# A delta-rule recurrence with eight heads of a direction in one chain instead of two chains of four

## The chip, the core and the metric

The kernel runs on one core of a Trainium2 chip. The core's engines are PE (matrix multiply, with the load of its weights, PEld, shown apart), DVE, ACT and POOL (elementwise work) and SP, which here only issues transfers. Each engine takes its instructions in the order in which they were written down, and they meet through semaphores. The metric is the device time of one execution in microseconds (us), and less is better.

## What is computed

The program is a small network: two mixed layers and two blocks more. The change touches one part of the first layer, a recurrence over 768 tokens (256 of context, 512 of image), run once forwards and once backwards, for eight heads of 64 values each. For each head and token the reference does this to a 64 x 64 state S:

```python
def step(S, inp):
    r_t, w_t, k_t, v_t, kk_t, a_t = inp
    sa = jnp.einsum('bhvk,bhk->bhv', S, kk_t)
    S = (S * w_t[:, :, None, :] - sa[..., None] * (kk_t * a_t)[:, :, None, :]
         + v_t[..., None] * k_t[:, :, None, :])
    return S, jnp.einsum('bhvk,bhk->bhv', S, r_t)
```

The outputs of both directions are added. Beside it the layer has a softmax attention with four heads, which needs nothing of the recurrence.

## The kernel before

The 768 tokens are cut into 12 chunks of 64, so a direction takes 12 steps. Within a step the token-by-token rule is turned into matrix products of 64 x 64. The part of a step that needs no state is the generator `local` (line 1286); the part that needs the state of the step before is `state` (line 1378). The eight heads of a direction stand as four pairs, with the two heads of a pair on partitions 0 to 63 and 64 to 127. A chain is one direction `d` and one group `g` of two pairs (four heads), so there are four chains, and a tile of a chain is 128 partitions by 2 x 64 columns.

`local` goes so: ACT takes two exponentials of the cumulated decay, DVE and POOL scale the inputs into `AR` and `BK` (lines 1301 to 1306), PE multiplies `BK` by `AR` into one PSUM bank, and DVE masks it first into `W`, then into `G` (lines 1321 to 1323). Then the inverse of a triangular matrix is built by levels: three rounds that make `X` (line 1327), and for each of two levels a product `LT` by `X` that DVE masks into `W` (line 1351), and three rounds that make `XT` (line 1360), with a transpose by the unit matrix before and after (`turn`). Every round is one group of matmuls (`both`: all heads of the chain, 64 x 64 each) whose result DVE or ACT carries from PSUM into SBUF, where the next group of the same chain reads it. In the trace a 64 x 64 matmul of float32 shows as two instructions, so a group of a chain is 8 instructions in it. `LT`, `W` and the other tiles that live for the whole stage are cut from three slots named `room`, PSUM tiles are named `m`, and the inputs come from DRAM (`rkv`) by one DMA for each chain and step.

The order of all this work is made by a planner (`Plan.run`, with costs that are written down in it). It holds a list of streams: the modulation matmuls (`pmod`) and the attention (`attn0`) with priority 0, the four `states` with 1, the four `locals_` with 2. A stream is run to its next `yield`; it is ready again 150 ns after the planned end of what it issued. The planner takes the ready stream of the best priority, and where none is ready, the one that will be so first. The attention is spread over the stage by `pace`, which lets its next part start 1,900 ns of planned time after the one before (lines 932 and 1032). A PSUM tile takes one of seven banks in turn, whatever its size (line 1256).

Of the kernel before, what the change touches and what calls it, by code (L numbers as in the profile page):

```python
# [17 lines left out]
P = 128  # L18
# [476 lines left out]
class Kern:  # L495
# [623 lines left out]
    def rwkv_cols(self, col, done):  # L1119
# [15 lines left out]
        self.rkv = self.dp.tile([12, 2, P, 5, 128], F32, name="rkv")  # L1135
# [31 lines left out]
        def head(h):  # L1167
# [34 lines left out]
            for n, t in enumerate((r, kx, v, kk, b)):  # L1202
                nc.sync.dma_start(self.rkv[:, h // 2, :, n, 64 * (h % 2) : 64 * (h % 2) + 64].rearrange("c p i -> p c i"), t.rearrange("p (c i) -> p c i", i=64))
# [10 lines left out]
    def rwkv_steps(self, rw, extra, qkv):  # L1214
# [5 lines left out]
        two = lambda m: m.unsqueeze(1).to_broadcast([P, 2, m.shape[1]])  # L1220
        I = self.mk[:, :64]
# [8 lines left out]
        mN = [two(mk(d, 192, 64)) for d in range(2)]  # L1230
        mW = [[None] + [mk(d, 128 + 128 * l, 128).rearrange("p (a b) -> p a b", a=2).unsqueeze(1).to_broadcast([P, 2, 2, 64]) for l in (1, 2)] for d in range(2)]

        E = [self.ident[:, j] for j in J]
        dg = [(d, g) for g in range(2) for d in range(2)]
# [6 lines left out]

        room = [self.slot("room", a=1)[:, 0, :] for _ in range(3)]
        ARs = {}
        for n, x in enumerate(dg):
            t = self.wp.tile([P, 1024], F32, tag=("whi", "wlo")[n % 2], name=self.nm("AR"), bufs=2)
            nc.gpsimd.memset(t, 0.0)
            ARs[x] = [t[:, a : a + 512].rearrange("p (a b) -> p a b", a=2) for a in (0, 512)]
        nc.gpsimd.memset(room[0], 0.0)
        LTs, Ws, KDs, ins = {}, {}, {}, {}
        for n, x in enumerate(dg):  # L1250
            t = [room[0][:, 768 * n + a : 768 * n + a + 256].rearrange("p (a b) -> p a b", a=2) for a in (0, 256, 512)]
            LTs[x], Ws[x] = t[:2], t[2]
            KDs[x] = [room[1][:, 512 * n + a : 512 * n + a + 256].rearrange("p (a b c) -> p a b c", a=2, b=2) for a in (0, 256)]
            ins[x] = room[2][:, 640 * n : 640 * n + 640].rearrange("p (n h i) -> p n h i", n=5, h=2)
# [5 lines left out]
        def pairs(dst, lhs, rhs, start=True, stop=True):  # L1260

            for h, j in HJ:
                mm(dst[J[j], h, :], lhs(h, j), rhs(h, j), start=start, stop=stop)
# [6 lines left out]
        def both(dst, lhs, rhs, **k):  # L1270

            for h, j in HJ:
                mm(dst[J[j], h, :], lhs[:, h, J[j]], rhs[:, h, :], start=True, stop=True)
# [6 lines left out]
        def ct(d, g, tag, shape, bufs=1):  # L1280
            return self.kp.tile([P] + shape, F32, tag=f"{tag}{d}{g}", name=self.nm(tag), bufs=bufs)

        def load(i, d, g):
            nc.scalar.dma_start(ins[d, g], self.rkv[order[d][i], g].rearrange("p n (h i) -> p n h i", h=2))

        def local(i, d, g):
# [4 lines left out]
            hs = slice(2 * g, 2 * g + 2)  # L1291
            r, kx, v, kk, b = (ins[d, g][:, n, :, :] for n in range(5))
            Dp = dp[d][i % 2][:, hs, :]
            Din, Dex = (Dp[:, :, 1:65], Dp[:, :, 0:64]) if d == 0 else (Dp[:, :, 0:64], Dp[:, :, 1:65])
            Dc = Dp[:, :, 64:65] if d == 0 else Dp[:, :, 0:1]
            nc.scalar.activation(Din, cum[d][:, hs, cs], AF.Exp, scale=-C0)
            Di = ct(d, g, "X", [2, 64], 2)
            nc.scalar.activation(Di, cum[d][:, hs, cs], AF.Exp, scale=C0)
            AR, BK = ARs[d, g][i % 2], ct(d, g, "BK", [2, 128])
            LT, W = LTs[d, g][i % 2], Ws[d, g]  # L1300
# [7 lines left out]
            UV = ct(d, g, "UV", [2, 2, 64], 2)  # L1308
# [7 lines left out]
            G = ct(d, g, "G", [2, 2, 128], 2)  # L1316
            gp = bank().rearrange("p (a b) -> p a b", a=2)
            for h, j in HJ:
                mm(gp[J[j], h, :], BK[:, h, J[j]], AR[:, h, :], start=True, stop=True)
            A = [slice(64, 128), slice(0, 64)]  # L1320
            for j in range(2):
                nc.vector.tensor_tensor(W[J[j], :, J[j]], gp[J[j], :, 64 + 64 * j : 128 + 64 * j], mN[d][J[j]], op=MUL)
            nc.vector.tensor_tensor(G, gp.rearrange("p a (b c) -> p a b c", b=2), mG[d], op=MUL)
            yield

            I2 = two(I)
            for it in range(3):
                ps = ps1()
                if it == 0:
                    both(ps, W, I2)  # L1330
                else:
                    both(ps, W, X)
                X = ct(d, g, "X", [2, 64], 2)
                nc.vector.tensor_tensor(X, I2, ps, op=SUB)
                if it == 0:
                    if i < 11:
                        load(i + 1, d, g)
                    for j in range(2):
                        nc.scalar.copy(LT[J[j], :, J[j]], G[J[j], :, j, A[j]])
                elif it == 1:  # L1340

                    KD = KDs[d, g][i % 2]
                    ps = bank()[:, :256]
                    for h, j in HJ:
                        mm(ps[J[j], h * P : (h + 1) * P], BK[:, h, J[j]], self.ident, start=True, stop=True)
                    nc.scalar.copy(KD.rearrange("p a b c -> p (a b c)"), ps)
                yield
            for l in (1, 2):
                ps = ps1()
                both(ps, LT, X)  # L1350
                nc.vector.tensor_tensor(W.rearrange("p a (b c) -> p a b c", b=2), ps.unsqueeze(2).to_broadcast([P, 2, 2, 64]), mW[d][l], op=MUL)
                if l == 1:
                    pt = ps1()
                    turn(pt, X)
                    XT = DT = ct(d, g, "XT", [2, 64], 3)
                    nc.scalar.copy(DT, pt)
                else:
                    DT = XT
                yield
                for it in range(3):  # L1360
                    ps = ps1()
                    both(ps, W, XT)
                    if it == 2 and l == 2:
                        for j in range(2):
                            nc.vector.tensor_tensor(LT[J[j], :, J[j]], DT[J[j]], ps[J[j]], op=SUB)
                    else:
                        XT = ct(d, g, "XT", [2, 64], 3)
                        nc.vector.tensor_tensor(XT, DT, ps, op=SUB)
                    yield
                if l == 1:  # L1370
                    pt = ps1()
                    turn(pt, XT)
                    X = ct(d, g, "X", [2, 64], 2)
                    nc.scalar.copy(X, pt)
                    yield
            parts[i, d, g] = (c, cs, Dc, AR, G, UV, KD, LT)

        def state(i, d, g):

            c, cs, Dc, AR, G, UV, KD, T = parts.pop((i, d, g))  # L1380
            hs = slice(2 * g, 2 * g + 2)
            s0 = S.get((d, g))

            ps = ps1()
            for h in range(2):
# [4 lines left out]
            R = ct(d, g, "R", [2, 64])  # L1390
# [7 lines left out]
            if i < 11:  # L1398
                ps = ps1()
                pairs(ps, lambda h, j: KD[:, h, j, :], lambda h, j: UV[:, h, j, :])  # L1400
                Sn = ct(d, g, "S", [2, 64], 2)
                if s0 is None:
                    nc.vector.tensor_tensor(Sn, ps, Dc.to_broadcast([P, 2, 64]), op=MUL)
                else:
                    nc.vector.tensor_tensor(Sn, s0, ps, op=ADD)
                    nc.vector.tensor_tensor(Sn, Sn, Dc.to_broadcast([P, 2, 64]), op=MUL)
                S[d, g] = Sn
                yield
            ps = ps1()
            for h in range(2):  # L1410
# [5 lines left out]
            if (c, g) in seen:  # L1416
                nc.vector.tensor_tensor(cum[0][:, hs, cs], cum[seen[c, g]][:, hs, cs], ps, op=ADD)
            else:
                nc.scalar.copy(cum[d][:, hs, cs], ps)
                seen[c, g] = d  # L1420
            ended[d, g] = i + 1
            yield

        def locals_(d, g):
            load(0, d, g)
            for i in range(12):
                yield Wait(lambda: ended.get((d, g), 0) >= i - 1)
                yield from local(i, d, g)

        def states(d, g):  # L1430
            for i in range(12):
                yield Wait(lambda: (i, d, g) in parts)
                yield from state(i, d, g)

        self.run((extra, 0), (self.attn0(qkv, bank), 0), *[(states(*x), 1) for x in dg], *[(locals_(*x), 2) for x in dg])
# [1087 lines left out]
```

## Time and profile before

| what | us |
|---|---|
| median of three timed runs (3727.8 to 3730.7) | 3727.83 |
| the profiled execution, as timed | 3725.59 |
| its span on the core | 3723.8 |
| the stage of the recurrence, from its first input DMA (301.5) to its last matmul (772.3) | 470.8 |
| PE, PEld, DVE, ACT and POOL busy in that stage | 433.6, 359.8, 384.1, 303.3, 139.0 |

The profile is one execution. Busy times count what an engine executes. Matmuls overlap, and their ends are modelled, so a busy PE may still have gaps between the starts of its matmuls; PEld, with one weight load for every matmul, shows more of them. All lines of the kernel go through a recording helper and stand as L245, so instructions are told apart by the names of their tiles: `XT<-XT,m` is the DVE operation that makes `XT` from PSUM, `m<-XT,room` the matmuls that read it next.

### The profile page before, as it was taken

How to read it: one execution, taken by the hardware profiler on the slowest of the kernel's cores; microseconds unless marked ns; L12 is line 12 of the kernel's file. 1: busy time of each engine (PE TensorE's matmuls, PEld its weight loads, DVE VectorE, ACT ScalarE, POOL GpSimd, SP SyncE). 2: the span in 40 equal slices, each digit the busy share in tenths (PEclk: the TensorE clock that was granted, in tenths of full speed). 3: DMA queues.
4: the chain of work that ended last, by engine and by line, in shares of the span. 5: the costliest groups of instructions: out<-in, count | busy, mean ns of one | idle time of the engine just before them, and what ended most of it. 6: DMA issues, size and time to landing. Idle time of an engine off the chain costs nothing.

```text
span 3723.8 us, 61572 instructions
## 1 busy us (share of the span) xinstructions
PE 3541.7 (95%) x25118; PEld 2940.9 (79%) x25118; DVE 2124.9 (57%) x3764; ACT 1539.6 (41%) x2992; POOL 652.1 (18%) x817
## 2 busy tenths in 40 slices
PE   7998998999999998888899989999999999999998
PEld 5786787888999997766788867777888777778886
DVE  5636787865333346588644465656554456565542
ACT  5425666634212214355432333554433245543331
POOL 3314232202000002443300030003110100031100
PEclk9999999999999999988999999999999999999999
DMA  5423311123333312111232232223333322233322
GB/s 205 115 81 134 121 53 35 36 91 112 125 108 125 102 63 86 54 35 35 91 99 98 97 104 71 66 74 102 96 96 101 123 68 68 69 104 95 98 96 89
DMA packets 128860, 337.11 MB, mean 91 GB/s; under 512 B 41537, under 2 KB 44609, under 8 KB 127425
## 3 DMA queue, kind: packets, MB, share of 16 engines
q1 hardware_dynamic: 113168, 297.31, 24.8%
q10 hardware_dynamic: 13584, 29.57, 2.5%
q0 software_dynamic: 1824, 6.29, 0.5%
q8 instruction: 198, 3.24, 0.4%
q14 instruction: 86, 0.70, 0.1%
HBM read 315.30 MB, written 17.83 MB: 89 GB/s over the span
## 4 chain that ended last, share of the span: by engine, by line
PE 67%; DVE 8%; POOL 2%; ACT 2%; issue 1%; DMA 0%; ACTq 0%; DVEq 0%; POOLq 0%
PE g L245 60%; PE m L245 6%; DVE t L245 3%; POOL t L245 1%; PE pmod L245 1%; DVE G L245 1%; DVE wlo L245 1%; DVE X L245 1%; ACT t L245 0%; DVE pk L245 0%; DVE QF L245 0%; ACT whi L245 0%; DVE KF L245 0%; POOL X L245 0%; ACT pk L245 0%
## 5 line engine op out<-in xcount | busy, mean ns | idle before, releaser
L245 PE MATMUL g<-pk,whi 128*128 128x512 f32 x3328 | 1083.5, 398 | 21.0 <-ACT t L245 11.2
L245 ACT CAST whi<-raw 128x1024 fp32r<-128x1024 f32 (+1 forms) x441 | 460.0, 1043 | 1248.9 <-PE g L245 1169.8
L245 PE MATMUL g<-H,whi 128*128 128x512 f32 (+2 forms) x2976 | 746.6, 359 | 19.6 <-ACT H L245 9.7
L245 DVE TENSOR_TENSOR wlo<-raw,whi 128x1024 fp32r<-128x1024 f32 (+1 forms) x414 | 511.4, 1235 | 427.5 <-ACT whi L245 423.0
L245 PEld LDWEIGHTS g<-pk,whi 128*128 128x128 f32 x3328 | 623.1, 190 | 161.1 <-ACT t L245 12.3
L245 PE MATMUL g<-pk,wlo 128*128 128x512 f32 x1824 | 718.3, 394 | 2.0 <-DVE wlo L245 2.0
L245 PEld LDWEIGHTS g<-H,whi 128*128 128x128 f32 x2976 | 516.3, 193 | 99.6 <-ACT H L245 13.0
L245 PE MATMUL g<-H,wlo 128*128 128x512 f32 (+2 forms) x1488 | 440.9, 354 | 11.2 <-POOL wlo L245 7.2
L245 PEld LDWEIGHTS g<-pk,wlo 128*128 128x128 f32 x1824 | 345.4, 189 | 77.0 <-DVE wlo L245 2.9
L245 PEld LDWEIGHTS g<-H,wlo 128*128 128x128 f32 x1488 | 262.6, 193 | 42.8 <-POOL wlo L245 8.8
L245 DVE SCALAR_TENSOR_TENSOR X<-g,mod,X 128x128 f32<-128x128 f32 (+3 forms) x320 | 162.9, 546 | 225.3 <-PE g L245 225.2
L245 PE MATMUL g<-hidh,whi 128*128 128x384 f32 (+2 forms) x896 | 276.1, 349 | 2.2 <-ACT hidh L245 1.3
L245 PE MATMUL g<-hidh,wlo 128*128 128x384 f32 (+2 forms) x896 | 275.1, 348 | 2.2 <-DVE wlo L245 2.1
L245 PE MATMUL g<-hidl,whi 128*128 128x384 f32 (+2 forms) x896 | 274.8, 347 | 0.2 <-DVE hidl L245 0.2
L245 POOL TENSOR_TENSOR t<-t,t 128x512 f32<-128x512 f32 (+3 forms) x60 | 79.8, 1336 | 598.2 <-ACT t L245 307.7
L245 POOL TENSOR_SCALAR t<-t,gain,mod 128x256 f32<-128x256 f32 (+3 forms) x56 | 54.0, 972 | 725.6 <-DVE t L245 725.1
L245 PEld LDWEIGHTS g<-hidh,whi 128*128 128x128 f32 x896 | 165.5, 189 | 19.6 <-issue 6.7
L245 PEld LDWEIGHTS g<-hidh,wlo 128*128 128x128 f32 x896 | 165.8, 189 | 14.3 <-DVE wlo L245 3.0
L245 PEld LDWEIGHTS g<-hidl,whi 128*128 128x128 f32 x896 | 166.0, 189 | 12.1 <-DVE hidl L245 0.5
L245 POOL TENSOR_TENSOR ssk<-ssk,t 128x512 f32<-128x512 f32 x37 | 66.7, 1807 | 581.6 <-ACT t L245 581.6
L245 ACT ACTIVATE t<-t 128x512 f32<-128x512 f32 (+5 forms) x179 | 98.2, 554 | 159.9 <-DVE t L245 157.6
L245 POOL TENSOR_TENSOR t<-t,rs 128x512 f32<-128x512 f32 x44 | 56.9, 1293 | 427.9 <-ACT t L245 427.9
(417 smaller groups left out, 5226.1 us busy)
## 6 DMA issues: line engine op xcount, KB each, us to landing
raw<-in_win_dram SPq DMA_DIRECT2D x131, 512.0 KB, 3.6
raw<-in_w_dram SPq DMA_DIRECT2D x130, 512.0 KB, 3.3
raw<-in_wup_dram SPq DMA_DIRECT2D x88, 512.0 KB, 3.6
mraw<-in_modw_dram SPq DMA_DIRECT2D x48, 512.0 KB, 5.8
raw<-in_modw_dram SPq DMA_DIRECT2D x32, 512.0 KB, 4.1
raw<-in_wda_dram SPq DMA_DIRECT2D x32, 512.0 KB, 3.6
room<-rkv ACTq DMA_DIRECT2D x48, 320.0 KB, 3.0
raw<-in_wout_dram SPq DMA_DIRECT2D x20, 512.0 KB, 3.3
```

The costliest lines, as they stand in the source:

```text
L245: r = f(*a, **k)
```

## The change

The group `g` is gone: a chain is a direction with all four pairs, so two chains of eight heads take the place of four chains of four heads. Tiles of a chain are 128 partitions by 4 x 64 columns, a group of a round is eight 64 x 64 matmuls (16 instructions in the trace), and DVE, ACT and POOL work on 256 columns at a time where they had 128. PE has the same matmuls as before, 19,583 as written, in another order. DVE has 486 instructions fewer (3,278 for 3,764), ACT 324 fewer (2,587 for 2,911, 24 of them DMAs), POOL 144 fewer (673 for 817). The input DMAs of the steps are 24 of 640 KB for 48 of 320 KB, and the DRAM tile `rkv` is laid out to match. Two things go beyond the width. The product of `BK` and `AR` for four pairs fills two banks, so it is done in two halves with a `yield` between. And `W` is masked from `G` in SBUF after both halves, where it was masked from PSUM before `G`.

```diff
-        self.rkv = self.dp.tile([12, 2, P, 5, 128], F32, name="rkv")
+        self.rkv = self.dp.tile([12, P, 5, 4, 64], F32, name="rkv")
...
-        dg = [(d, g) for g in range(2) for d in range(2)]
...
-        ps1 = lambda: bank()[:, :128].rearrange("p (a b) -> p a b", a=2)
-        HJ = [(h, j) for h in range(2) for j in range(2)]
+        ps1 = lambda: bank()[:, :256].rearrange("p (a b) -> p a b", a=4)
+        HJ = [(h, j) for h in range(4) for j in range(2)]
...
-            G = ct(d, g, "G", [2, 2, 128], 2)
-            gp = bank().rearrange("p (a b) -> p a b", a=2)
-            for h, j in HJ:
-                mm(gp[J[j], h, :], BK[:, h, J[j]], AR[:, h, :], start=True, stop=True)
+            G = ct(d, "G", [4, 2, 128], 2)
             A = [slice(64, 128), slice(0, 64)]
+            for a in (0, 2):
+                gp = bank().rearrange("p (a b) -> p a b", a=2)
+                for h, j in HJ[:4]:
+                    mm(gp[J[j], h, :], BK[:, a + h, J[j]], AR[:, a + h, :], start=True, stop=True)
+                nc.vector.tensor_tensor(G[:, a : a + 2], gp.rearrange("p a (b c) -> p a b c", b=2), mG[d], op=MUL)
+                if a == 0:
+                    yield
             for j in range(2):
-                nc.vector.tensor_tensor(W[J[j], :, J[j]], gp[J[j], :, 64 + 64 * j : 128 + 64 * j], mN[d][J[j]], op=MUL)
-            nc.vector.tensor_tensor(G, gp.rearrange("p a (b c) -> p a b c", b=2), mG[d], op=MUL)
-            yield
-
-            I2 = two(I)
+                nc.vector.tensor_tensor(W[J[j], :, J[j]], G[J[j], :, j, A[j]], mN[d][J[j]], op=MUL)
+            yield
+
             for it in range(3):
                 ps = ps1()
-                if it == 0:
-                    both(ps, W, I2)
-                else:
-                    both(ps, W, X)
-                X = ct(d, g, "X", [2, 64], 2)
-                nc.vector.tensor_tensor(X, I2, ps, op=SUB)
+                both(ps, W, X if it else I4)
+                X = ct(d, "X", [4, 64], 2)
+                nc.vector.tensor_tensor(X, I4, ps, op=SUB)
...
-                        XT = ct(d, g, "XT", [2, 64], 3)
+                        XT = ct(d, "XT", [4, 64], 3)
                         nc.vector.tensor_tensor(XT, DT, ps, op=SUB)
...
-        self.run((extra, 0), (self.attn0(qkv, bank), 0), *[(states(*x), 1) for x in dg], *[(locals_(*x), 2) for x in dg])
+        self.run((extra, 0), (self.attn0(qkv, bank), 0), *[(states(d), 1) for d in range(2)], *[(locals_(d), 2) for d in range(2)])
```

All other edits of the diff drop `g` from names and indices, or put 4 where a shape had 2.

Two places show what it does to the order. The first is PE in the later rounds of a step, about half-way through the stage. `m1_` is a PSUM tile, and a result in `XT_` or `X_` has a number one above that of the PSUM tile it was made from. Before:

```order
L245 MATMUL m1_1339_6899<-XT_1331_6866,room_341_2419 64x64 x4
L245 MATMUL m1_1341_6906<-XT_1333_6875,room_341_2419 64x64 x4
L245 MATMUL m1_1343_6913<-XT_1335_6882,room_341_2419 64x64 x4
L245 MATMUL m1_1345_6920<-XT_1338_6897,room_341_2419 64x64 x4
L245 MATMUL m1_1347_6928<-XT_1340_6904,room_341_2419 64x64 x4
L245 MATMUL m1_1349_6935<-XT_1342_6911,room_341_2419 64x64 x4
L245 MATMUL m1_1351_6942<-ident_70,XT_1344_6918 64x64 x4
```

And after the change, at the same point of a step:

```order
L245 MATMUL m1_955_6057<-XT_942_6019,room_341_2419 64x64 x8
L245 MATMUL m1_959_6073<-XT_952_6050,room_341_2419 64x64 x8
L245 MATMUL m1_961_6086<-XT_956_6066,room_341_2419 64x64 x8
L245 MATMUL m1_963_6099<-XT_960_6082,room_341_2419 64x64 x8
L245 MATMUL m1_965_6110<-ident_70,XT_962_6095 64x64 x8
L245 MATMUL m1_967_6123<-ident_70,XT_964_6108 64x64 x8
L245 MATMUL m1_969_6134<-X_966_6119,room_341_2419 64x64 x8
L245 MATMUL m1_970_6144<-X_968_6132,room_341_2419 64x64 x8
L245 MATMUL m1_971_6156<-XT_962_6095,room_341_2419 64x64 x8
L245 MATMUL m1_973_6167<-XT_964_6108,room_341_2419 64x64 x8
```

Before, three groups of the other chains stand between a group (`m1_1339`) and the one that reads its result (`XT_1340`); after, there is one group between (`m1_961` between `m1_959` and the reader of `XT_960`), and it is twice as long.

The second place is DVE where `G` and `W` are made, in `room`. Before:

```order
L245 TENSOR_TENSOR AR_344_2422<-room_343_2421,dp00_2411 64x2x64 x2
L245 TENSOR_TENSOR room_341_2419<-m1_1247_6473,c_mk_501 64x2x64 x2
L245 TENSOR_TENSOR G_1246_6472<-m1_1247_6473,c_mk_501 128x512
L245 TENSOR_TENSOR S_1252_6506<-S_1095_5766,m1_1251_6501 128x128
L245 TENSOR_TENSOR S_1254_6514<-S_1102_5806,m1_1253_6509 128x128
```

And after the change:

```order
L245 TENSOR_TENSOR G_1009_6423<-m1_1010_6424,c_mk_501 128x512
L245 TENSOR_TENSOR X_1014_6447<-c_mk_501,m1_1013_6438 128x256
L245 TENSOR_TENSOR AR_345_2423<-room_343_2421,dp01_2412 64x4x64
L245 TENSOR_TENSOR AR_347_2427<-room_343_2421,dp11_2414 64x4x64 x2
L245 TENSOR_TENSOR G_1009_6423<-m1_1020_6480,c_mk_501 128x512
L245 TENSOR_TENSOR room_341_2419<-G_1009_6423,c_mk_501 64x4x64 x2
```

`W` came first, straight from the product in PSUM; now it comes last, behind both halves of `G`.

After the stage, the engines' orders are those of before but for some 130 rows of PE's (of about 12,700) in the last block, where the planner puts some matmuls of the gate columns to other places beside the attention.

## Rows read from the trace of the kernel before

**Rows 1.** The page: the span, and the input DMAs of the steps.

```profile
span 3723.8 us, 61572 instructions
...
room<-rkv ACTq DMA_DIRECT2D x48, 320.0 KB, 3.0
```

**Rows 2.** Windows: busy PE, PEld, DVE, ACT, POOL; clock; DMA share, GB/s.

```profile
301.50:772.30 470.80, 433.62 (x9257) 359.79 (x9256) 384.08 (x1233) 303.30 (x977) 139.00 (x323) 0.99 0.26 83
301.50:326.00 24.50, 17.72 (x128) 9.05 (x128) 14.25 (x33) 10.50 (x31) 19.62 (x43) 0.86 0.51 170
326.00:752.00 426.00, 398.36 (x8618) 334.11 (x8612) 355.66 (x1154) 281.33 (x918) 119.39 (x280) 1.00 0.24 75
```

**Rows 3.** Timeline of PE: start, length, what (groups of a round).

```profile
504.14 0.43 PE L245 MATMUL m<-XT,room 128*64 128x64 f32 x8
504.37 0.43 PE L245 MATMUL m<-X,room 128*64 128x64 f32 x8
504.60 0.43 PE L245 MATMUL m<-ident,X 128*64 128x64 f32 x8
504.84 1.13 PE L245 MATMUL m<-XT,room 128*64 128x64 f32 x32
```

**Rows 4.** Timeline: a group that waits for ACT, and DVE behind it.

```profile
756.48 0.26 ACT L245 COPY XT<-m 128x128 f32<-128x128 f32 x1
...
756.79 0.45 PE L245 MATMUL m<-XT,room 128*64 128x64 f32 x8 [0.59 <-ACT XT L245]
...
757.36 0.29 DVE L245 TENSOR_TENSOR XT<-XT,m 128x128 f32<-128x128 f32 x1 [0.84 <-PE m L245]
```

**Rows 5.** Timeline: a long attention instruction on DVE ahead of a round's.

```profile
501.93 1.18 DVE L245 SCALAR_TENSOR_TENSOR t<-t,rs,t 128x768 f32<-128x768 f32 x1 [0.41 <-POOL t L245]
...
503.04 0.27 DVE L245 TENSOR_TENSOR XT<-XT,m 128x128 f32<-128x128 f32 x1
...
503.36 0.45 PE L245 MATMUL m<-XT,room 128*64 128x64 f32 x8 [1.07 <-DVE XT L245]
```

**Rows 6.** Lines by shape, DVE in the stage (busy us, mean ns, idle before).

```profile
L245 DVE TENSOR_TENSOR XT<-XT,m 128x128 f32<-128x128 f32 x240 | 61.2, 282 | 11.0 <-PE m L245 8.5
L245 DVE TENSOR_TENSOR room<-m,c_mk 128x256 f32<-128x256 f32 x96 | 39.2, 416 | 3.5 <-PE m L245 3.0
...
L245 DVE TENSOR_TENSOR G<-m,c_mk 128x512 f32<-128x512 f32 x48 | 33.2, 692 | 1.0
...
L245 DVE TENSOR_REDUCE mx<-t 128x1 f32<-128x768 f32 x32 | 29.6, 945 | 6.4 <-ACT t L245 6.4
...
L245 DVE SCALAR_TENSOR_TENSOR t<-t,rs,t 128x768 f32<-128x768 f32 x16 | 16.9, 1059 | 0.6 <-POOL t L245 0.4
```

**Rows 7.** Waits of PE's weight loads in the stage (total us, times, longest).

```profile
PEld m L245 <- DVE XT L245: 7.5, 14, 1.2
PEld m L245 <- DVE X L245: 7.3, 9, 1.7
PEld m L245 <- DVE room L245: 6.4, 14, 0.9
PEld m L245 <- POOL BK L245: 6.4, 3, 4.4
PEld m L245 <- ACT XT L245: 6.2, 10, 1.8
```

**Rows 8.** Timeline of PE: its first wait in the stage.

```profile
314.66 1.94 PE L245 MATMUL m<-AR,BK 128*64 128x256 f32 x8 [4.22 <-POOL BK L245]
```

**Rows 9.** Lines by shape, ACT in the stage.

```profile
L245 ACT COPY room<-m 128x256 f32<-128x256 f32 x48 | 17.7, 368 | 11.3 <-PE m L245 10.7
...
L245 ACT COPY X<-m 128x128 f32<-128x128 f32 x48 | 12.6, 266 | 28.1 <-PE m L245 27.9
```

**Rows 10.** Lines by shape, POOL in the stage.

```profile
L245 POOL TENSOR_TENSOR BK<-room,X 64x128 f32<-64x128 f32 x96 | 46.5, 484 | 48.9 <-ACT X L245 36.7 <-PE m L245 7.2
...
L245 POOL TENSOR_TENSOR k<-t,t 128x512 f32<-128x512 f32 x1 | 1.3, 1276 | 0.1
```

More of the change, by code (lines that the diff above doesn't have):

```diff
@@ L1219, in rwkv_steps @@
         J = [slice(0, 64), slice(64, 128)]
-        two = lambda m: m.unsqueeze(1).to_broadcast([P, 2, m.shape[1]])
-        I = self.mk[:, :64]
+        four = lambda m: m.unsqueeze(1).to_broadcast([P, 4, m.shape[1]])
+        I4 = four(self.mk[:, :64])
         mk = lambda d, a, w: self.mk[:, 64 + 512 * d + a : 64 + 512 * d + a + w]
@@ L1229, in rwkv_steps @@
         mG = [windows(mk(d, 0, 128)) for d in range(2)]
-        mN = [two(mk(d, 192, 64)) for d in range(2)]
-        mW = [[None] + [mk(d, 128 + 128 * l, 128).rearrange("p (a b) -> p a b", a=2).unsqueeze(1).to_broadcast([P, 2, 2, 64]) for l in (1, 2)] for d in range(2)]
+        mN = [four(mk(d, 192, 64)) for d in range(2)]
+        mW = [[None] + [mk(d, 128 + 128 * l, 128).rearrange("p (a b) -> p a b", a=2).unsqueeze(1).to_broadcast([P, 4, 2, 64]) for l in (1, 2)] for d in range(2)]
         E = [self.ident[:, j] for j in J]
-        dg = [(d, g) for g in range(2) for d in range(2)]
         dp = [[self.kp.tile([P, 4, 65], F32, name=f"dp{d}{j}") for j in range(2)] for d in range(2)]
@@ L1268, in turn, with both @@
                 mm(dst[J[j ^ flip], h, :], src[:, h, :], E[j], start=True, stop=True)
-        def both(dst, lhs, rhs, **k):
+        def both(dst, lhs, rhs):
             for h, j in HJ:
@@ L1278, in rwkv_steps, with ct, load, local @@
         ended = {}
[L1280 to L1286, printed above, removed]
+        def ct(d, tag, shape, bufs=1):
+            return self.kp.tile([P] + shape, F32, tag=f"{tag}{d}", name=self.nm(tag), bufs=bufs)
+        def load(i, d):
+            nc.scalar.dma_start(ins[d], self.rkv[order[d][i]])
+        def local(i, d):
             c = order[d][i]
             cs = slice(c * 64, c * 64 + 64)
-            hs = slice(2 * g, 2 * g + 2)
-            r, kx, v, kk, b = (ins[d, g][:, n, :, :] for n in range(5))
-            Dp = dp[d][i % 2][:, hs, :]
+            r, kx, v, kk, b = (ins[d][:, n, :, :] for n in range(5))
+            Dp = dp[d][i % 2]
             Din, Dex = (Dp[:, :, 1:65], Dp[:, :, 0:64]) if d == 0 else (Dp[:, :, 0:64], Dp[:, :, 1:65])
             Dc = Dp[:, :, 64:65] if d == 0 else Dp[:, :, 0:1]
[L1296 to L1300, printed above, removed]
+            nc.scalar.activation(Din, cum[d][:, :, cs], AF.Exp, scale=-C0)
+            Di = ct(d, "X", [4, 64], 2)
+            nc.scalar.activation(Di, cum[d][:, :, cs], AF.Exp, scale=C0)
+            AR, BK = ARs[d][i % 2], ct(d, "BK", [4, 128])
+            LT, W = LTs[d][i % 2], Ws[d]
             for j in range(2):
@@ L1306, in local @@
                 nc.gpsimd.tensor_tensor(BK[J[j], :, J[1 - j]], kx[J[j]], Di[J[j]], op=MUL)
-            UV = ct(d, g, "UV", [2, 2, 64], 2)
+            UV = ct(d, "UV", [4, 2, 64], 2)
             ps = ps1()
@@ L1340, in local @@
                 elif it == 1:
-                    KD = KDs[d, g][i % 2]
-                    ps = bank()[:, :256]
+                    KD = KDs[d][i % 2]
+                    ps = bank()
                     for h, j in HJ:
@@ L1354, in local @@
                     turn(pt, X)
-                    XT = DT = ct(d, g, "XT", [2, 64], 3)
+                    XT = DT = ct(d, "XT", [4, 64], 3)
                     nc.scalar.copy(DT, pt)
@@ L1372, in local, with state @@
                     turn(pt, XT)
-                    X = ct(d, g, "X", [2, 64], 2)
+                    X = ct(d, "X", [4, 64], 2)
                     nc.scalar.copy(X, pt)
                     yield
[L1376 to L1382, printed above, removed]
+            parts[i, d] = (c, cs, Dc, AR, G, UV, KD, LT)
+        def state(i, d):
+            c, cs, Dc, AR, G, UV, KD, T = parts.pop((i, d))
+            s0 = S.get(d)
             ps = ps1()
-            for h in range(2):
+            for h in range(4):
                 for j in range(2):
@@ L1389, in state @@
                     mm(ps[J[j], h, :], AR[:, h, 64 + 64 * j : 128 + 64 * j], s0[:, h, :], start=False, stop=True)
-            R = ct(d, g, "R", [2, 64])
+            R = ct(d, "R", [4, 64])
             nc.scalar.copy(R, ps)
@@ L1399, in state @@
                 ps = ps1()
-                pairs(ps, lambda h, j: KD[:, h, j, :], lambda h, j: UV[:, h, j, :])
-                Sn = ct(d, g, "S", [2, 64], 2)
+                for h, j in HJ:
+                    mm(ps[J[j], h, :], KD[:, h, j, :], UV[:, h, j, :], start=True, stop=True)
+                Sn = ct(d, "S", [4, 64], 2)
                 if s0 is None:
-                    nc.vector.tensor_tensor(Sn, ps, Dc.to_broadcast([P, 2, 64]), op=MUL)
+                    nc.vector.tensor_tensor(Sn, ps, Dc.to_broadcast([P, 4, 64]), op=MUL)
                 else:
                     nc.vector.tensor_tensor(Sn, s0, ps, op=ADD)
-                    nc.vector.tensor_tensor(Sn, Sn, Dc.to_broadcast([P, 2, 64]), op=MUL)
-                S[d, g] = Sn
+                    nc.vector.tensor_tensor(Sn, Sn, Dc.to_broadcast([P, 4, 64]), op=MUL)
+                S[d] = Sn
                 yield
             ps = ps1()
-            for h in range(2):
+            for h in range(4):
                 for j in range(2 if s0 is not None else 0):
```

52 lines of the change are left out of this document (25 added, 27 removed).

## The prediction

> **What bounds the kernel now.** I read the page first for the span and the transfers [rows 1], then the windows of the one stage that the change touches [rows 2]. There the reader is to see two engines near their limit: in 470.8 us PE is busy for 433.6 and DVE for 384.1, 92% and 82%, and in its start alone (301.5 to 326) for much less. PE's busy time flatters it, since the tails of matmuls are in it; its weight loads fill 359.8 us, so 111.0 us have none.
>
> Next come the rounds, from the timeline. Groups that have what they need start 0.23 us apart: 504.14, 504.37, 504.60, 504.84, and the four that follow (32 instructions, 1.13 us to the end of the last, of which 0.20 is its tail) keep the stride [rows 3]. So a round of four chains costs PE 4 x 0.233 = 0.93 us. The loop of one chain is seen where PE had to wait [rows 4, 5]. A group runs 0.45 us to the end of its last matmul (756.79 to 757.24), DVE starts 0.12 later (757.36), works 0.28 [rows 6], and PE starts 0.05 after its operand is there (503.31 to 503.36; 756.74 to 756.79). Together 0.90 us, just under the 0.93 that the round takes anyway: four chains hide one chain's loop, with nothing to spare.
>
> Last I read who keeps PE waiting. DVE's three kinds of result (XT, X and W in `room`) take 21.2 us, ACT's XT 6.2, POOL's BK 6.4 [rows 7], 4.2 of it in one wait at the start [rows 8]. Part of this is not load but order: a 1.18 us instruction of the attention stands on DVE ahead of a round's XT, and PE idles 1.07 us [rows 5]. There are 48 such of about 1 us on DVE (32 + 16) [rows 6], and the change leaves them all. The granted clock is 1.00 in the middle [rows 2], the higher level (2.4 GHz), and I price no change of it.
>
> **The change part by part.** *PE's work* stays: the same matmuls. A group is 16 instructions, 0.465 us in the stride above, and two chains make 0.93 us a round, as four did.
>
> *The loop grows.* The second 8 instructions end 0.23 later, at 0.68. DVE then works on 128x256, 0.416 where the row of that shape is [rows 6]; ACT 0.368 [rows 9]. So a loop is 0.68 + 0.12 + 0.416 + 0.05 = 1.27 us over DVE, 1.22 over ACT, while PE has 0.93 to do: 0.34 or 0.29 short, unless another stream's group stands between. The order tells where none does. Of the 267 groups that read X or XT made from a result of their chain, I count 124 with one group or less between (92 over DVE, 32 over ACT); before, 7 of 529 had fewer than three. A gap paid by one chain is cover for the other's next group, so one of two pays: 46 x 0.34 + 16 x 0.29 = 20.3 us. Where W of the second level is made (128x512 for the chain, 0.692 as for that shape [rows 6]) the loop is 1.54, 0.61 short; 18 of 24 have one group between: 9 x 0.61 = 5.5. Before, W cost 0.416 there, a loop of 1.04 against 0.93: 9 x 0.11 = 1.0. Net +24.7 us. Bounds: 0, if blocked instructions have shifted the chains apart anyway, and 51.6, if every place pays alone (92 x 0.34 + 32 x 0.29 + 18 x 0.61). I take 24.7, since the order shows long runs of strict alternation.
>
> *DVE and ACT are relieved.* Two instructions of 128 columns take 2 x 282 ns, one of 256 takes 416: 148 ns saved for each of DVE's 486 removed, 72 us, which leaves 312, 66% of the stage. ACT saves 2 x 266 - 368 = 164 ns for each of 300, 49 us of 303. Neither ends the stage, so only the waits they cause count. Those that I read there are 27.4 us (21.2 + 6.2): from nothing to all of it. The largest single ones (1.2 to 1.8 us) are as long as the attention's instructions, which stay, so I take somewhat under half, 12. And in a round of four, DVE's four XT are 4 x 0.282 = 1.13 us against PE's 0.93, now 2 x 0.416 = 0.83: 0.20 a round at most, over 6 such rounds in 12 steps 14 us. Seven groups in a row keep the full stride all the same [rows 3], so I take 4, near the lower end, 0.
>
> In this trace DVE at 82% is near its limit, yet PE's waits for it are 21.2 of 470.8 us [rows 2, 7]. The Trainium skill (Perfetto Trace Analysis, Optimizing Scalar/DVE Operations) says that larger operations help throughput where an engine is saturated, but that where Scalar and Vector are not saturated and still cause bubbles on other engines, breaking instructions up may let work finish sooner. By its first half the sum would be the first rival below; by its second half none of the 16 us is given back, and the sum is +25.8.
>
> *The start.* The first product waits for POOL's BK [rows 8]. A POOL instruction of twice the width has no row; from 484 ns for 128 columns and 1276 for 512 [rows 10] comes 484 + 264 = 748 ns, an estimate. Four of them stand before the first product, 3.0 us for 1.9: +1.1, between 0 (DVE is late too) and 1.9 (twice the 484).
>
> *W behind G.* After the last half of the product come G (0.692) and two masks of 256 columns (0.416 each): about 1.9 us from PE's last instruction to the reader of W. At three places of the order where I added up PE's groups between (attention, state, the other chain), they came to 2.7, 2.8 and 2.9 us, so I take 0; uncovered it is the third rival.
>
> *Transfers.* A step's input lands in 3.0 us [rows 1]; with 640 KB at most twice that, and it is asked for early in the step before, some 39 us (470.8 / 12) long: 0. The DMAs issue on ACT's queue, 24 fewer, which is a gain I leave out. *The last block*: 1% of PE's rows after the stage change places; a tenth of that share of the 2,950 us there is 3, of either sign, for the range alone.
>
> Sum: 24.7 + 1.1 - 12 - 4 = +9.8 us. On the profiled execution (3725.6, of which 3723.8 span) that is 3735.4. The median of the runs is 2.2 above this execution, so the forecast is 3737.6, rounded to 3738.
>
> **The rivals.** *DVE was the bound.* If waiting for DVE and ACT is a matter of their load, 66% in place of 82% ends all 27.4 and all 14, and the gaps of the rounds are half filled by state and attention groups that arrive late: 12.4 + 1.1 - 27.4 - 14 = -27.9, 3700. For it: DVE and PE are both above 80%, and stalls of in-order engines feed each other. Against it: the full stride [rows 3], and the 48 long instructions.
>
> *Gain and loss cancel.* Only half of the gaps is paid, because the alternation in the order is broken in time by each long instruction: 12.4 + 1.1 - 16 = -2.5, 3725, within 0.2% of before. For it: a stall of 1 us behind one long instruction is on record [rows 5], and it puts the waiting chain out of step. Against it: two chains that wait for one another fall back into step within a round.
>
> *W is not covered.* If DVE comes to the masks late (the state's and the other chain's instructions of 0.42 us stand among them), half of the 1.9 us shows in each of 24 chain steps: 23 us on top of the 9.8, 3761. It decides from the point where the groups between fall under 1.9 us or DVE is 1 us behind. For it: the path through G is the one that the change lengthens by rewriting and not by width. Against it: the cover counted above.
>
> That the change does nothing is no rival: PE's order alone shows that it does.
>
> **How the numbers follow.** Forecast (3738) 0.33, W uncovered 0.12, cancel 0.30, DVE bound 0.25. About 0.2%, 7.5 us, is what a measurement of this kernel can tell from no change. So slower is 0.33 + 0.12 = 0.45, within 0.30, faster 0.25. The range runs from 3704, near the first rival, to 3764, just over the third: what lies beyond, all gaps paid alone (+52) or the gain of the first rival without any gap, is about 2 in 10. The forecast's own range is 3736 to 3750, if between 4 and 18 us are given back where I took 16.
>
> **What would show it.** In the profile after, `XT<-XT,m` should stand as 128x256 x120 at about 0.42 us, and DVE's busy time in the stage near 312 us. In the runs of alternating groups, PE should start a pair every 1.27 us and not every 0.93, with waits for DVE XT and ACT X or XT of about 0.3 us, some 60 of them. The long waits behind the attention's instructions should still be there. The stage should end some 10 us later. I am wrong if the pairs come in the 0.93 stride, if PE's waits for DVE all but vanish, or if the stage before or after this one changes its length by more than 3 us.

## The result, and the profile after

The changed kernel takes 3759.2 us (median of 4 runs, 3752.5 to 3764.6), the kernel before 3727.8: a ratio of 1.0083, with a 95% interval of 1.0063 to 1.0103. So it is slower, as forecast, and inside the range; but the forecast was 3738. The loss is 31 us by the medians, and 37.1 us between the two profiled executions (3762.6 against 3725.6), where the sum had +9.8. Most of what follows is about the 27 us between.

All of it lies in the stage. The last matmul of the recurrence starts at 808.9 us, before at 772.3: 36.5 us later. From there to the end it is 2,952.0 us, before 2,951.5. (Where the text below says how much earlier or later a stage ends, it is this matmul's start, in the profiled execution.)

The windows of the stage and of its start, columns as in [rows 2]:

```profile
301.20:809.00 507.80, 451.11 (x9258) 362.80 (x9256) 345.64 (x748) 265.95 (x677) 120.40 (x179) 0.98 0.22 76
301.20:326.00 24.80, 17.72 (x112) 9.10 (x110) 14.41 (x24) 10.74 (x27) 17.47 (x27) 0.86 0.48 165
```

PE does the same work (362.8 us of weight loads, 359.8 before) in 37 us more. DVE is relieved, but by 38 us and not 72: 345.6 for 384.1.

DVE's lines by shape, which answer to [rows 6]:

```profile
L245 DVE TENSOR_TENSOR XT<-XT,m 128x256 f32<-128x256 f32 x120 | 49.2, 416 | 18.4 <-PE m L245 16.9
L245 DVE TENSOR_TENSOR G<-m,c_mk 128x512 f32<-128x512 f32 x48 | 33.0, 689 | 38.0 <-PE m L245 37.7
L245 DVE TENSOR_TENSOR room<-m,c_mk 128x512 f32<-128x512 f32 x48 | 32.6, 684 | 11.3 <-PE m L245 10.9
```

The durations are those of the forecast. New is the idle time: DVE waits 38.0 us for PE ahead of G (1.0 before), 18.4 ahead of XT (11.0): the two engines now wait for each other in turn.

Who keeps PE's weight loads waiting, beside [rows 7] (its line `issue`, idle time with no wait that the profile shows, is put first):

```profile
PEld m L245 <- issue: 18.3, 47, 1.7
```

and after the change:

```profile
PEld m L245 <- issue: 30.7, 66, 2.7
PEld m L245 <- DVE XT L245: 21.3, 38, 2.0
PEld m L245 <- DVE room L245: 15.0, 21, 2.1
...
PEld m L245 <- DVE X L245: 6.1, 10, 1.2
PEld m L245 <- POOL BK L245: 5.7, 1, 5.7
PEld pmod L245 <- DMA raw<-in_modw_dram: 5.2, 5, 3.3
PEld m L245 <- ACT XT L245: 3.9, 6, 1.2
```

Waits for DVE's XT are up from 7.5 to 21.3 us and those for W and LT in `room` from 6.4 to 15.0. A line that the forecast never looked at has grown, from 0.8 to 5.2 us: the modulation's matmuls (`pmod`, weights streamed into `raw`) wait for their transfers. The largest line, `issue`, is up from 18.3 to 30.7, but it doesn't carry the loss: in the two kernels below that lose little or nothing it is 32.0 and 28.5. The start, beside [rows 8], went as worked out:

```profile
315.71 1.82 PE L245 MATMUL m<-AR,BK 128*64 128x256 f32 x6 [5.57 <-POOL BK L245]
```

Here is one stretch of the rounds, first PE (the last row is cut off by the window):

```profile
764.47 0.69 PE L245 MATMUL m<-XT,room 128*64 128x64 f32 x16
764.99 0.64 PE L245 MATMUL m<-X,room 128*64 128x64 f32 x16
766.18 1.00 PE L245 MATMUL m<-XT,room 128*64 128x64 f32 x22 [0.56 <-DVE XT L245]
```

and DVE at that time:

```profile
764.00 0.42 DVE L245 TENSOR_TENSOR XT<-XT,m 128x256 f32<-128x256 f32 x1
764.78 1.02 DVE L245 SCALAR_TENSOR_TENSOR t<-t,rs,t 128x768 f32<-128x768 f32 x1 [0.36 <-POOL t L245]
765.72 0.41 DVE L245 TENSOR_TENSOR XT<-XT,m 128x256 f32<-128x256 f32 x1
```

The group at 764.47 waits to be followed by its chain's next at 766.18, 1.71 us later: its XT stands behind an attention instruction of 1.02 us, and between them PE has only the other chain's group, 0.5 us long. Before, three groups stood there.

To compare kernels, I took from each trace how much later each matmul starts than the stride of its kind after the one ahead of it, and added that up over the stage by the operand it begins with. This is PE's idle time, in us:

```
                       ahead of XT   X    first reader of W  modulation  all   stage's end
before                    27.2     13.5         4.4             4.9      88.5     772.3
changed                   49.6     19.0        11.4            13.6     125.3     808.9
W from PSUM               48.0     22.4         2.6             9.4     114.1     797.2
loop in halves            27.1     13.2        12.2            11.2      95.9     779.1
both                      21.6     17.4         3.4             7.5      83.2     765.9
```

The matmuls themselves are worth 375 us in each. Of the 36.8 us of idle time that the change adds, 27.9 stand ahead of XT and X, 7.0 ahead of the first reader of W, 8.7 at the modulation; the others gave back 6.8.

### The profile page after: what moved, and what is told of

It reads as the page before. It is cut to its first block, busy times and chain, and to the rows that moved or that the text cites. A ratio compares the mean times of both kernels' runs of the same rounds, so it can differ in the third digit from the quotient of the medians.

```text
span 3760.9 us, 60328 instructions
## 1 busy us (share of the span) xinstructions
PE 3558.2 (95%) x25118; PEld 2942.2 (78%) x25118; DVE 2085.9 (55%) x3278; ACT 1500.8 (40%) x2692; POOL 634.7 (17%) x673
## 3 DMA queue, kind: packets, MB, share of 16 engines
q1 hardware_dynamic: 113168, 297.31, 24.7%
## 4 chain that ended last, share of the span: by engine, by line
PE 67%; DVE 7%; POOL 2%; ACT 1%; issue 1%; DMA 0%; ACTq 0%; DVEq 0%; POOLq 0%
PE g L245 60%; PE m L245 6%; DVE t L245 3%; POOL t L245 1%; PE pmod L245 1%; DVE G L245 1%; DVE wlo L245 1%; DVE X L245 0%; ACT t L245 0%; DVE pk L245 0%; ACT whi L245 0%; POOL X L245 0%; DVE KF L245 0%; DVE yg L245 0%; ACT pk L245 0%
## 5 line engine op out<-in xcount | busy, mean ns | idle before, releaser
L245 PE MATMUL g<-H,whi 128*128 128x512 f32 (+2 forms) x2976 | 743.5, 358 | 21.3 <-ACT H L245 10.8
L245 PEld LDWEIGHTS g<-pk,wlo 128*128 128x128 f32 x1824 | 345.6, 189 | 76.9 <-DVE wlo L245 2.9
L245 ACT COPY t<-m 128x512 f32<-128x512 f32 (+3 forms) x220 | 97.5, 483 | 81.3 <-PE m L245 80.0
```

What stands on the lines that cost most here:

```text
L245: r = f(*a, **k)
```

## The experiments

**W from PSUM** undoes one part: W is masked from the product, not from G.

```diff
 for a in (0, 2):
     ...
+    for j in range(2):
+        nc.vector.tensor_tensor(W[J[j], a : a + 2, J[j]], gp[J[j], :, 64 + 64 * j : 128 + 64 * j], mN[d][J[j], 0:2], op=MUL)
     nc.vector.tensor_tensor(G[:, a : a + 2], gp.rearrange("p a (b c) -> p a b c", b=2), mG[d], op=MUL)
-    if a == 0:
-        yield
-for j in range(2):
-    nc.vector.tensor_tensor(W[J[j], :, J[j]], G[J[j], :, j, A[j]], mN[d][J[j]], op=MUL)
-yield
+    yield
```

> The changed kernel with one part undone: W is masked from each half of the product in PSUM, ahead of G (two masks of 64x128 a half), not from G in SBUF behind both halves. Theory 'W is late': in the changed kernel PE stands still 11.4 us ahead of the first reader of W (m<-c_mk,room), before 4.4; with W made first the path from product to W falls from 0.69 + 2 x 0.45 to 2 x 0.29 us, those idle times return to about 4 us, and the time falls by some 7 us from 3759 to about 3752. Rival 'only moved': PE meets the next late operand (G, LT, XT) instead, and the time stays within 3 us of 3759.

Measured: 3752.4 us, 1.0074 (1.0059 to 1.0089) times the kernel before run beside it. The idle time ahead of W's first reader falls to 2.6 us, and the stage ends 11.7 us earlier. By the times alone, 1.0074 against 1.0083, it isn't told apart from nothing; the profiles say that W was late, and is no longer.

**The loop in halves** keeps two chains, but inside the inversion makes each result for two head pairs at a time.

```diff
+HV = [slice(0, 2), slice(2, 4)]
 ...
+def both2(lhs, rhs, fn):
+    for s in HV:
+        ps = half()
+        for h, j in HJ[:4]:
+            mm(ps[J[j], h, :], lhs[:, s.start + h, J[j]], rhs[:, s.start + h, :], start=True, stop=True)
+        fn(s, ps)
 ...
-ps = ps1()
-both(ps, W, XT)
-XT = ct(d, "XT", [4, 64], 3)
-nc.vector.tensor_tensor(XT, DT, ps, op=SUB)
+Xo, XT = XT, ct(d, "XT", [4, 64], 3)
+both2(W, Xo, lambda s, ps: nc.vector.tensor_tensor(XT[:, s], DT[:, s], ps, op=SUB))
```

> The changed kernel with two chains still, but inside the inversion (X, W of the second level, XT, and the two transposed copies) every result is made in two halves of two head pairs: 8 matmuls into one bank, then DVE or ACT on 128x128 (or 128x256 for W), then the other half. All else (AR, BK, UV, G, KD, state, loads) stays 256 wide. Theory 'the loop': the first half of the next group can start 0.45 + 0.12 + 0.28 + 0.05 = 0.90 us after its own start, PE has 0.93 us a round, so the idle time ahead of XT and X (68.6 us after, 40.7 before) falls by about 28 us, and the time goes from 3759 to about 3731, though DVE has some 240 instructions more. Rival 'load and order': the loss comes from elsewhere (long attention instructions, modulation, W), the halves only add DVE work (some 30 us busy), and the time stays at 3755 or above.

Measured: 3728.8 us, 1.0011 (1.0002 to 1.0021); the stage ends 29.8 us earlier. The idle time ahead of XT and X is back at 40.3 us (40.7 before the change). The waits of PE's weight loads in it:

```profile
PEld m L245 <- DVE XT L245: 8.5, 16, 1.1
PEld m L245 <- ACT XT L245: 6.5, 9, 1.2
...
PEld m L245 <- DVE room L245: 5.5, 10, 1.9
PEld m L245 <- DVE X L245: 4.1, 7, 0.9
```

and its window:

```profile
301.30:779.10 477.80, 438.02 (x9256) 359.90 (x9254) 364.47 (x1035) 269.77 (x725) 116.33 (x179) 0.99 0.24 82
```

Two things follow. In this order the loop is the largest part of the loss. And this kernel tests the relief by itself, though with half of DVE's (19.6 us less busy, for 38) and with W still late: its loop is that of the kernel before, ACT is 33.5 us less busy, and yet the four waits from which I took 12 us add up to 24.6, where they were 27.4.

**Both edits together:**

> The two edits together: results of the inversion in halves, and W from PSUM ahead of G. If the loop and the late W are separate losses, they add: 3759 - 28 - 7 = about 3724, some 4 us under the kernel before, what remains of the loss being the modulation's 9 us, and what is won being DVE's and ACT's wider instructions in AR, BK, UV and the state. Rival 'nothing in relief': it ends no lower than the kernel before, 3728 to 3740.

Measured: 3713.7 us (10 runs), 0.9974 (0.9965 to 0.9984): faster than either kernel. The stage ends 42.9 us before that of the changed kernel, so the two add up (29.8 + 11.7), and 6.4 us before that of the kernel before. The two edits are thus enough to undo the whole loss, with nothing done to the modulation. Only these 6.4 us are credited to the wide instructions that are left; in the profiled execution another 8.4 come after the stage, which the edits don't touch; there the other kernels with this stage whole differ by -4.4 to +5.8 us. The four waits of above add up to 22.2 us.

**The chains alone**, attention and modulation put behind them:

```diff
-self.run((extra, 0), (self.attn0(qkv, bank), 0), *[(states(d), 1) for d in range(2)], *[(locals_(d), 2) for d in range(2)])
+self.run(*[(states(d), 1) for d in range(2)], *[(locals_(d), 2) for d in range(2)])
+self.run((self.attn0(qkv, bank), 0), (extra, 0))
```

(and the modulation's first instruction ordered behind the last one of the recurrence, which holds it there).

> The kernel before (four chains of 128 columns), with the attention and the modulation put behind the recurrence and not between its groups; all work is done, only later, so the whole is longer and only the stretch of the recurrence (first product m<-AR,BK to the last m<-G,UV) is read. Its matmuls are worth 287 us at the stride of groups. Theory 'the loop': the chain's loop of 0.90 us is covered by the round of 0.93, so the stretch is some 330 us (287, 7 for the start, some 35 of idle times).

> The same for the changed kernel (two chains of 256 columns). Theory 'the loop': in 12 rounds of each of 12 steps both chains wait, 0.34 us a round over DVE and 0.29 over ACT, so with nothing to put between the stretch is some 45 us (144 x 0.31) plus up to 20 for W longer than that of the four chains alone, about 390 to 395; pairs of groups come every 1.27 us. Rival 'it is the company': the chains by themselves lose little, since states of one direction stand beside rounds of the other, and what was lost is where long attention instructions and modulation hit two chains at once: the difference is under 20 us.

Measured: 333.1 us for the four chains, 363.7 for the two: 30.7 us, between the two theories, nearer to the loop's (each is a single execution, as are the next two). The waits of PE's weight loads, first four chains:

```profile
PEld m L245 <- DVE room L245: 14.5, 26, 1.7
PEld m L245 <- DVE X L245: 8.5, 17, 1.0
...
PEld m L245 <- DVE XT L245: 0.7, 1, 0.7
```

then two:

```profile
PEld m L245 <- DVE room L245: 21.5, 39, 0.9
PEld m L245 <- DVE XT L245: 16.2, 57, 0.6
PEld m L245 <- DVE X L245: 14.3, 19, 1.4
```

One wait for XT against 57: this is the loop that was covered and no longer is. By the count of idle time, some 28 of the 32 us more stand ahead of XT. Where groups of the inversion alternate without anything between, a chain's next group starts 1.21 us (median of 213) after its last in the two-chain kernel, and 0.93 us (median of 440) in the other. With the attention between, the same medians are 1.42 (161) and 1.07 (308).

**The modulation taken out** of the stage, the attention left in:

> The kernel before with the modulation alone (128 matmuls that read streamed weights, 18.4 us of PE) put behind the recurrence; attention stays between. Only the stage is read. Expected: the stage is some 20 us shorter than in the kernel before (470.8), about 450, since the modulation waits for its transfers for only 1 us there.

> The same for the changed kernel. Theory 'modulation pays': in the changed kernel PE waits 9 us for the modulation's transfers, since its matmuls stand closer behind one another in PE's order; without it the difference between the two stages falls from 37 to about 28 us. Rival 'cover': the modulation's waits lie where PE would wait for the chains anyway; the difference stays 37 or grows, since the modulation's matmuls also filled gaps of the rounds.

Measured: the stages end at 756.4 and 772.4 us, 16.0 apart for 36.5; 2.0 of the 16 lie ahead of the stage, whose first input DMA is at 301.4 and 303.4. The theory's direction holds, but its size doesn't: not 9 but 20 us of the loss go with the modulation. (The 9 counted waits twice, 5.2 us of weight loads and 4.1 of the same matmuls.) In what is left of the loss, by the count of idle time, W weighs as much as the loop: some 11 us each more ahead of W's first reader and ahead of XT and X. Since the modulation's 128 matmuls also change where everything else falls, the next edit leaves them in and only has them read a table in SBUF, so that the modulation's values are others:

```diff
-nc.tensor.matmul(ps[o : o + 2, :], self.cs[:, k, :], w[:, q * 512 : q * 512 + 512], ...)
+nc.tensor.matmul(ps[o : o + 2, :], self.cs[:, k, :], (self.mk if l == 0 else w)[:, q * 512 : q * 512 + 512], ...)
```

> The changed kernel, whose 128 modulation matmuls of this stage read a table that lies in SBUF and not the streamed weights (the transfers still run, nobody reads them; the modulation's values are therefore others, the work the same). Theory 'modulation waits': PE's idle time ahead of these matmuls (13.6 us, 9.3 of it for transfers) falls to about 4, and the stage from 507.8 to about 498, the time from 3759 to about 3750. Rival 'modulation sets the order': as in the pair without modulation, 23 of the 37 us go, to about 3736, because the groups of the chains fall elsewhere. Third: the waits are cover for the chains, and the time stays within 3 us.

> The kernel before with its modulation matmuls of this stage reading a table in SBUF and not the streamed weights, as in the changed kernel of that kind, whose stage ended 20.5 us earlier for it. In the kernel before PE stands still 4.9 us ahead of these matmuls, 0.8 of it for transfers. If the modulation's waits belong to the change, this kernel gains 5 us at most and 15 to 20 of the 36.5 us are theirs. If both kernels lose by the modulation's place in the order, it gains 10 to 20 us as well, and the change's own share of it is 0 to 10.

Measured: the changed kernel goes to 3739.8 us, 1.0037 (1.0021 to 1.0053), its stage ends 20.5 us earlier, 18.4 of it by the fourth of the twelve steps. The kernel before doesn't move: 1.0000 (0.999 to 1.001), stage's end 0.5 us later. So some 17 us by the times, 20 by the profiles, go with this edit in the changed kernel and none in the other. That they are the waits' is not shown, for the edit also moves the modulation in PE's order, and not alike in the two: it is done at 400 us for 477 in the changed kernel, and at 465 as before in the other. By the count, PE's idle time ahead of these matmuls falls from 13.6 to about 2 us in the one, and goes from 4.9 to about 6 in the other. In the changed kernel the worst place looks like this (its PE, the transfers' issues, and the transfers of 355 to 370 us with their time to landing):

```profile
366.05 1.87 PE L245 MATMUL pmod<-raw,c2s 128*2 128x512 f32 x2 [3.17 <-DMA raw<-in_modw_dram]
```

```profile
358.30 0.33 ACTq L245 DMA_DIRECT2D room<-rkv  x1
...
359.62 0.80 SPq L245 DMA_DIRECT2D raw<-in_modw_dram  x2
...
362.06 0.33 ACTq L245 DMA_DIRECT2D room<-rkv  x1
```

```profile
room<-rkv ACTq DMA_DIRECT2D x2, 640.0 KB, 5.2
raw<-in_modw_dram SPq DMA_DIRECT2D x2, 512.0 KB, 6.7
```

Two inputs of 640 KB meet two strips of the modulation's weights; these land after 6.7 us, where 3.7 is their median in the stage (4.1 before the change), and PE, which takes its matmuls in order, stands still for both chains. The other waits (0.2 to 0.7 us) have no input beside them: there the matmul merely comes too soon after its strip was asked for, 398.6 to 401.8 us for one. Direct waits are 5.2 us of weight loads (0.8 before), and 9.5 us by the time from each of these matmuls to the next (32.9 for 23.4). What the remaining 10 are is open: place and transfer aren't told apart.

**Where the planner puts the attention**, by its pace alone (line 932; 1800 or 2000 ns a segment for 1900):

> The changed kernel with the attention's pacing at 1800 ns a segment for 1900: nothing but the order of PE's groups is changed, by a little. If the size of the loss is a property of the loop, of W and of the modulation, the time stays within 4 us of 3759. If it depends on where the planner happens to put the attention between the rounds, it moves by 5 to 15 us, either way.

> The same at 2000 ns a segment: within 4 us of 3759 if the loss is a property of the chains, 5 to 15 us away, either way, if it is where the planner puts the attention.

> The kernel before at 2000 ns a segment. If 1900 fits the four chains by a choice of numbers that the two chains only inherit, this kernel loses 5 us or more against 3728; if the order hardly matters, it stays within 4 us.

Measured: 3754.1 and 3753.7 us (1.0073, 1.0050 to 1.0096, and 1.0075, 1.0052 to 1.0098) for the changed kernel, its stage ending 9.0 and 6.2 us earlier; 3734.4 us, 1.0021 (1.0010 to 1.0033), for the kernel before. By the times the changed kernel moves by less than its interval. The kernel before loses 0.2%, 4.5 us of it in the stage: 1900 suits four chains better than its neighbour does. Placement alone is worth 4 to 9 us of a stage, which is also how far the differences above, each from one order, can be trusted.

The waits of PE's weight loads in the changed kernel's stage, at 1800:

```profile
PEld m L245 <- DVE XT L245: 20.0, 37, 2.2
PEld m L245 <- DVE room L245: 13.8, 23, 2.1
...
PEld pmod L245 <- DMA raw<-in_modw_dram: 0.3, 1, 0.3
```

and at 2000, where none is for the modulation's strips:

```profile
PEld m L245 <- DVE XT L245: 18.2, 34, 2.1
PEld m L245 <- DVE room L245: 16.7, 24, 2.4
```

The waits for XT and `room` are there at each pace; the modulation's waits for its strips belong to the one order at 1900, and without them the kernel still loses 0.7%. How the loss divides is a matter of the order too: by the count of idle time, some 58 us (1800) and 51 us (2000) stand ahead of XT and X, where it was 68.6, and some 17 and 20 ahead of W's first reader, where it was 11.4; the kernel before has some 37 and 3 at 2000, for 40.7 and 4.4.

## Why the prediction came out as it did

- *The loop* was right as a mechanism. 1.27 us was worked out and 1.21 measured for the chains alone, 0.93 and 0.93 for four; +24.7 in the sum, 29.8 when it is undone, 27.9 by the idle time ahead of XT and X. That the size fits as well, with 46 + 16 places that pay on the assumption that one of two does, is in part luck: at a pace of 2000 the same idle time is only some 14 us more than in the kernel before at that pace.
- *The relief of DVE and ACT* (16 us) failed, twice. Its size: the 148 ns saved for each instruction is that of XT's shape, and the others save less (durations times counts fall from 434.0 to 372.8 us, by 61); and it came from recorded durations, which overlap on DVE. The lines of DVE before add up to 421.9 us, while the window has 384.1 busy [rows 2]; after, XT starts at 757.72 and the next instruction at 758.05, 0.33 us later, though XT is recorded with 0.41:

```profile
757.72 0.41 DVE L245 TENSOR_TENSOR XT<-XT,m 128x256 f32<-128x256 f32 x1
758.05 0.68 DVE L245 TENSOR_TENSOR room<-m,c_mk 128x512 f32<-128x512 f32 x1
```

  So the relief was 38 us of DVE's time and not 72. The Trainium skill (Perfetto Trace Analysis, Optimizing Scalar/DVE Operations) says that the profiled latency is about twice an instruction's data-access overhead, since the half that acknowledges the write overlaps with the next instruction; the trace agrees that records overlap, by 0.08 us here, and no run shows the factor of two. And its worth: in the changed kernel the waits rose by 18.9 (21.3 + 6.1 + 15.0 + 3.9 against 27.4), and with the loop restored they fell by 2.8 us, not 12. That 2.8 is no price of the relief, for placement moves these waits by more: the kernel before has 16.2 us of them at a pace of 2000, in a stage that is 4.5 us longer. PE waited for results that were late by order and by length, not for an engine that was full. The second half of that section of the Trainium skill, weighed in the prediction and given no part in the sum, is the better rule here: breaking the loop's instructions up again brought 0.7%.
- *W behind G* was taken as covered, at 0. It cost 7.0 us ahead of its first reader, 11.7 when undone, and some 18 by the idle time if both kernels have a pace of 2000. One place where it shows: the product runs 506.7 to 508.7 us, but DVE is just then in two attention reductions, and G and the masks come after them.

```profile
506.80 1.93 DVE L245 TENSOR_REDUCE mx<-t 128x1 f32<-128x768 f32 x2
508.65 0.16 DVE L245 TENSOR_SCALAR mx<-mx 128x2 f32<-128x2 f32 x1
508.71 1.28 DVE L245 TENSOR_TENSOR G<-m,c_mk 128x512 f32<-128x512 f32 x2
509.91 0.86 DVE L245 TENSOR_TENSOR room<-G,c_mk 64x256 f32<-64x256 f32 x2
```

```profile
510.47 0.30 PE L245 MATMUL m<-c_mk,room 128*64 128x64 f32 x2 [1.78 <-DVE room L245]
```

  The cover had been counted in PE's groups, on the assumption that DVE is free when the product ends. The third rival named this condition; its price of 23 us was twice what undoing W gave back, so that its 3761 is near to the result is luck: its sum gives back 16 us in relief that did not come.
- *Transfers at 0* asked only whether a chain's own input comes in time. It does, in 4.0 us for 3.0. It didn't ask who else uses the transfers, nor that a new order of PE also moves the matmuls that read streamed weights. In the measured order they wait 5.2 us directly, and by the count 8.7 us more idle time than before stands ahead of them; the 17 to 20 us of the run with the table in SBUF hold a change of place as well. At the other two paces the direct waits are 0.3 and 0, so these are a cost of one order and not of the wider chains.
- *The start* (+1.1) was 1.05 (1.35 from the stage's first DMA, which comes 0.3 us earlier), and what follows the stage changed by 0.5 us at the end, where up to 3 were allowed.

The sum came out 27 us short, then, because it gave back 16 us of relief that did not come, and put nothing for W and for what else the new order moves. The shares don't add up to 36.5: undone one by one, the loop, W and the modulation give 62 us. The loop and W do add (41.5 singly, 42.9 together, the whole loss and 6.4 more), so the modulation's 20 is no share of its own. What remains open is what each is worth in general. Alone, the two chains lose 30.7 us; with the attention between, which may fill some of their gaps, 16.0; with the modulation as well, 36.5; each of these is from one execution in one order. The middle figure, good to within what placement is worth, is what the sum of +9.8 was about, with W in it.

Of the signs, XT at 128x256 x120 and 0.42 us came, and the long waits behind attention instructions stayed; XT's and X's waits were fewer and longer than the 60 of 0.3 us (54 of DVE and ACT, 31.3 us in all), for what 0.3 us leaves short becomes 1 us behind a long instruction. That DVE was the bound is refuted: it has 68% of the stage and PE waits for it more than ever.

## What to carry to other kernels

Before chains are merged, set the loop of one (matmuls, eviction, DVE's or ACT's instruction, way back) against what PE has to do in a round of all the others: here 0.90 against 0.93 held, 1.21 against 0.93 didn't, and fewer instructions in the loop bought nothing that showed. Wide instructions belong where no loop waits for them (operands, state, transfers), narrow ones inside it: that version was the fastest. And when a change moves the order of an in-order engine, price also what it places beside the chains and what that waits for, and try a second order before putting a size to one part: here one number of the planner moved the stage by 4 to 9 us and the shares by more.

## What the runs showed of the hardware that was not expected

POOL's products of AR and BK slow DVE's, which like them read both operands from SBUF. In the changed kernel's stage, the 57 of DVE's 96 whose record overlaps one of POOL's products take 675 ns in the mean, the other 39 take 431 (401 for 97 and 284 for 95 in the kernel before); the same shape with one operand from PSUM takes 418:

```profile
L245 DVE TENSOR_TENSOR BK<-room,X 64x256 f32<-64x256 f32 x48 | 28.0, 583 | 5.0 <-ACT X L245 4.2
L245 DVE TENSOR_TENSOR AR<-room,dp 64x256 f32<-64x256 f32 x48 | 27.3, 569 | 8.5 <-ACT dp L245 7.0 <-DMA room<-rkv 1.0
...
L245 DVE TENSOR_TENSOR room<-XT,m 64x256 f32<-64x256 f32 x48 | 20.1, 418 | 10.3 <-PE m L245 9.5
```

The Trainium skill (SBUF — State Buffer, Who interferes with whom) says that a DVE instruction with two SBUF inputs contends with a GpSimd instruction that reads SBUF, and that one with at most one such input, outside the 2-port modes, doesn't; the trace agrees with the first half (the masks `room<-G,c_mk`, both operands in SBUF, take 692 ns in the 6 cases that overlap a product of POOL's and 418 in the other 42) and with the second (XT, with one operand from PSUM, takes 410 ns in 20 cases that overlap and 417 in the other 100; before, 279 in 70 and 283 in 170). Whether POOL's products are slowed in turn is not shown: 797 ns with overlap and 736 without after the change, but 461 and 478 before. No run here parted the two engines, so what it costs the stage stays open.
